# k's first tile among the products of the first stage, and the first modulation's sums shared out anew

## The chip, the cores and the metric

The kernel runs on one core of one Trainium2 chip. The metric is the time of one execution in microseconds on the device (us): the median of the timed runs. A core has TensorE (matmuls, below PE; its weight loads PEld), VectorE (DVE), ScalarE (ACT), GpSimd (POOL) and SyncE (SP, which here only issues transfers from memory). Each engine works through its own list in order and waits where something it needs is not there. Matmuls add up in PSUM, which has 8 banks; everything else lies in SBUF.

## The reference

One decoder block on x of 512 tokens by 1024 features, all in float32: a modulation vector from c, an RMS norm with scale and shift, nine projections of it, retention over q, k, v with rotary phases, a short gated convolution of b, c and u, a gated merge, and an FFN. What bears on this change:

```python
mod = silu(c) @ ada_w + ada_b                       # 6 x 1024: shift, scale, gate (mixer), the same (FFN)
h = rmsnorm(x, norm_mix_g) * (1 + sc_m) + sh_m      # 512 x 1024
q, k, v, g_ret, b_cv, c_cv, u_cv, g_a, g_b = split(h @ w_in, 9)
q, k = rope(q), rope(k)                             # cos and sin of positions * inv_freq
u = c_cv * u_cv                                     # then three taps, times b_cv
```

## The kernel before

*Products in three parts.* Every matrix product is made of reduced-precision parts: a float32 tensor is split into a high part (`_h`, a cast on ScalarE) and a low part (`_l`, a subtraction, mostly on VectorE), and three products are added, low by high, high by low, and high by high. For the normed input these are `Hh` and `Hl`, for weights `w_.._h` and `w_.._l`.

*The first stage* (lines 330 to 512) runs while the weights of the modulation still arrive. x comes in four tiles, is squared and scaled, and is turned by TensorE (`tx`) into `xT`, features on partitions: eight slices of 128 features. A slice can be modulated only when the sums of `ada_w` over c for its features are there. So the features go in pairs of slices j = 0, 2, 4, 6. `ada_load("m", j)` brings the shift and scale columns of the pair as 8 transfers of 256 KB, and `w_load(j)` the pair's rows of w_in for the first two column tiles of c, u and b.

*The modulation of a pair.* Its 8 raw rows are weighted with silu(c). `ada_sum` and `some_sums` do it on VectorE, one instruction for a row of 512 values (`acc_m`); four small matmuls with ones then add over the partitions (`mod_m<-ones,acc_m`). For pair 0, `mod_first` lets TensorE take rows 0, 1, 2, 3 and 7 directly from the raw weights, and VectorE sums rows 4 to 6. `mod_cols` makes shift `s_m` and scale `a_m` from the result; `h_hi` applies them on ScalarE, twice, once rounded into `Hh` and once in full; `h_lo` makes `Hl` on VectorE.

*The products of slice k* (`products(k)`) are 18 matmuls: six groups (two tiles each of c, u and b), each with three parts. All six groups stay in PSUM from slice 0 to slice 7: four banks called `acc`, two called `pv`; two more, `aux`, hold the modulation sums. `busy(n)` are matmuls whose result nobody reads.

*What sets the order.* In this stage the order is written out by hand: with `strict`, each engine's instruction is issued behind the one before it in the program. In the loop over j, 8 products of slice j-1 come ahead of pair j's sums and 10 behind them.

*Behind the stage* a scheduler orders each engine's list. v of the first head pair is projected (`value_proj`), then k (`proj`, two tiles of 24 matmuls), q and the gate. VectorE meanwhile computes the rotary phases (`rotary`, tiles `fr`, `fy`, `ft`); ScalarE makes their sines and cosines (`ropeC`, `ropeS`) behind a table load; `rope` applies them to k and q; then come the scores (`st`) of retention, which need the split k and q. For the second head pair the low part of v's weights is made by GpSimd. Raw weights lie in three buffers (`raw`), split ones in four each (`hi`, `lo`), and projections in the four `acc` banks, each in rotation.

Of the kernel before, what the change touches and what calls it, by code (L numbers as in the profile page):

```python
# [70 lines left out]
def block_kernel(ctx, tc, x, c, positions, ada_w, ada_b, norm_mix_g, w_in, conv_w, ret_w_out,  # L71
# [143 lines left out]
    def mod_cols(f, j, n, pt):  # L215

        r1 = R_ADA + ADA["sh_" + f] // P + j
        g0 = (R_GM if f == "m" else R_GF) + j
        for k in range(j, j + n):
            i = k - j  # L220
            vec.scalar_tensor_tensor(mod["a_" + f][:, k:k + 1], pt[:, n + i:n + i + 1],
                                     vecs[0][:, g0 + i:g0 + i + 1], mod["b_" + f][:, k:k + 1],
                                     ALU.mult, ALU.add)
            if k == j:
                vec.tensor_tensor(mod["s_" + f][:, j:j + n], pt[:, 0:n], vecs[0][:, r1:r1 + n],
                                  ALU.add)
# [8 lines left out]
    def mod_vecs(f, j, a=None):  # L235

        pt = aux(f"mod_{f}{j}")
        a = ada_sum(ada_raw.pop((f, j)), 4 * P, f"{f}{j}") if a is None else a
# [3 lines left out]
        mod_cols(f, j, 2, pt)  # L242


    def half_ss(part, s, h, name):
# [62 lines left out]
    def x_load():  # L308
        for t in range(NT):
            xt = wp.tile([P, 2, S], F32, tag="hi", name=f"x_{t}")  # L310
            xs[t] = [xt[:, h] for h in range(2)] + [xt.rearrange("p h n -> p (h n)")]
            load_raw.last = sync.dma_start(xs[t][2], x[0, t * P:(t + 1) * P, :])

    def w_load(k):
        for n in "cub":
            w_raw[n, k] = scr(f"w_{n}0_{k}", F32, [P, 2, 2 * P])
            load_raw.last = sync.dma_start(
                w_raw[n, k], wi[k * P:(k + 2) * P, COL[n]:COL[n] + 2 * P].rearrange(
                    "(k p) n -> p k n", p=P))

    pe.strict = pool.strict = act.strict = vec.strict = sync.strict = True
# [33 lines left out]
    mod01 = []  # L355

    def mod_first(k, tiles=(0, 1)):

        for j in tiles:
            for i in range(2):  # L360
                c0 = 2 * i * P + j * P
                mm(mod01[j][:, i:i + 1], lhsT=ada_raw["m", 0][k][:, c0:c0 + P], rhs=cs[:, k:k + 1],
                   start=k == 0 and i == 0, stop=False)

    def mod_sums(a, j):
        for i in range(2):
            c0 = 2 * i * P + j * P
            mm(mod01[j][:, i:i + 1], lhsT=a[:, c0:c0 + P], rhs=ones32[:, 0:1],
               start=False, stop=i == 1)
# [14 lines left out]
    transpose(tr[:, 0:P], rows, ident)  # L384
    x_squares(3)
    rows_by_feature(tr)
    mod01 += [aux(f"mod_m{j}") for j in range(2)]
    mod_first(0)
    x_scaled(2)
    busy(1)  # L390
    x_by_feature(1, 0, act.copy)
    x_by_feature(1, 1, vec.tensor_copy)
    mod_first(1)
    busy(1)
    mod_first(2)
# [12 lines left out]

    grp = [(n, i) for n in "cub" for i in range(2)]
    gps = {}  # L410
    for i, g in enumerate(grp):
        gps[g] = acc(f"p_{g[0]}0{g[1]}") if i < 4 else pv(f"p_{g[0]}0{g[1]}")
    wt, raws = {}, {}
    hist = []
    hlast = []

    def w_hi(n, k):
        raws[n, k] = w_raw.pop((n, k))
        wt[n, k] = [slot(f"w_{n}0_{k}_{z}", F32R, [P, 2, 2 * P]) for z in "hl"]
# [54 lines left out]
    busy(2)
    mod_first(7, (1,))
    mod_sums(a, 1)
    mod_cols("m", 1, 1, mod01[1])
    w_lo("u", 0)
# [154 lines left out]
    def proj(src, col, Ah, Al, name, eng=None):  # L633
        raw = load_raw(src, 0, KT, col, 2 * P, "w_" + name)
        for i in range(2):
            wh, wl = split(raw[:, :, i * P:(i + 1) * P], [P, KT, P], f"w_{name}{i}", eng)
            yield i, fm_gemm(acc(f"p_{name}{i}"), wh, wl, Ah, Al)
            tick()

    def gate_proj(p):  # L640
        for i in range(2):
            gate_split(p, i)
            wh, wl = gate_w.pop((p, i))
            yield i, fm_gemm(acc(f"p_g{p}{i}"), wh, wl, Hh, Hl)
            tick()
# [65 lines left out]
    for p in range(H // 2):  # L711
        kk, qq, vv, gg = {}, {}, {}, {}
        for i, pt in value_proj(p, pool if p == 1 else None):
            value(pt, f"v{p}{i}", vv, i)
        if p == 0:
            rope_tables()
        for i, pt in proj(wi, COL["k"] + 2 * p * P, Hh, Hl, f"k{p}"):
            kk[i] = rope(pt, f"k{p}{i}")
        for i, pt in proj(wi, COL["q"] + 2 * p * P, Hh, Hl, f"q{p}"):
            qq[i] = rope(pt, f"q{p}{i}")  # L720
        retention(p, kk, qq, vv, gg)
        for i, pt in gate_proj(p):
            gg[i] = slot(f"g{p}{i}")
            act.activation(gg[i], pt, AF.Silu)
# [296 lines left out]
```

## Time and profile before

| | us |
|---|---|
| median of 3 runs | 973.99 (972.45 to 975.49) |
| the profiled execution | 971.54 |
| its span, first to last instruction | 969.7 |
| TensorE busy in the span | 954.5 (98%) |
| VectorE busy | 558.7 (58%) |
| ScalarE busy | 340.0 (35%) |
| GpSimd busy | 15.2 (2%) |
| TensorE's mean granted clock | 0.995 of full speed |

Busy shares are averages over the whole span. Matmuls are pipelined, so the time of one as shown (0.39 us) is longer than the distance between the starts of two. The stage that the change touches is the first 62 us.

### The profile page before, as it was taken

What the parts mean: (1) busy time and instruction counts of PE and PEld (TensorE: products, weight loads), DVE (VectorE), ACT (ScalarE), POOL (GpSimd) and SP (SyncE); (2) the same over time, 40 slices, a digit from 0 to 9 for tenths busy, and PEclk for the clock granted to TensorE, in tenths of its full rate; (3) what the DMA queues carried; (4) which work ended last, traced back from release to release, by engine and by line L of the source; (5) the groups of instructions that cost most, each with busy time, mean ns of one, the idle gap of its engine ahead of it and who ended that gap; (6) DMA issues with size and microseconds to landing.
All of it is one profiled execution on the core that took longest, in us unless ns stands there. A gap on an engine that the chain in (4) does not pass through costs nothing.

```text
span 969.7 us, 11383 instructions
## 1 busy us (share of the span) xinstructions
PE 954.5 (98%) x4651; PEld 807.2 (83%) x4651; DVE 558.7 (58%) x836; ACT 340.0 (35%) x502; POOL 15.2 (2%) x22
## 2 busy tenths in 40 slices
PE   8899999999999999999999998999999999999997
PEld 8788989888888888888888887988888888888886
DVE  4888875959775755554574458356533433333354
ACT  7434434444543423222233336422322122222223
POOL 2001000000000000000000002000000000000000
PEclk9999999999999999999999999999999999999999
DMA  9953332141322146764553541235423222331302
GB/s 310 312 167 109 98 98 98 55 142 41 102 87 87 59 129 192 218 184 153 174 174 115 188 131 55 95 115 166 157 90 128 87 87 88 118 121 66 109 1 87
DMA packets 107956, 120.98 MB, mean 125 GB/s; under 512 B 3636, under 2 KB 95840, under 8 KB 107904
## 3 DMA queue, kind: packets, MB, share of 16 engines
q1 hardware_dynamic: 107680, 120.08, 39.3%
q8 instruction: 36, 0.59, 0.3%
q0 software_dynamic: 224, 0.18, 0.1%
q14 instruction: 16, 0.13, 0.0%
HBM read 118.15 MB, written 2.10 MB: 124 GB/s over the span
## 4 chain that ended last, share of the span: by engine, by line
PE 95%; DVE 2%; ACT 1%; DMA 1%; issue 1%; SPq 0%; ACTq 0%; DVEq 0%
PE p_fu L64 12%; PE p_fg L64 12%; PE dn L64 12%; PE p_v L64 5%; PE p_ga L64 5%; PE p_k L64 5%; PE p_q L64 5%; PE p_g L64 5%; PE p_gb L64 5%; PE p_yb L64 4%; PE p_ya L64 4%; PE mix L64 4%; PE p_u L64 3%; PE p_b L64 3%; PE p_c L64 3%; PE y L64 2%
## 5 line engine op out<-in xcount | busy, mean ns | idle before, releaser
L64 PE MATMUL p_fu<-Gl,w_fu_h 128*128 128x512 f32 (+1 forms) x192 | 71.4, 372 | 0.0
L64 PE MATMUL p_fu<-Gh,w_fu_l 128*128 128x512 f32 (+1 forms) x192 | 71.3, 371 | 0.0
L64 PE MATMUL p_fu<-Gh,w_fu_h 128*128 128x512 f32 (+1 forms) x192 | 71.3, 371 | 0.0
L64 PE MATMUL dn<-w_dn_h,fa_l 128*128 128x512 f32 (+1 forms) x176 | 67.5, 384 | 0.0
L64 PE MATMUL dn<-w_dn_l,fa_h 128*128 128x512 f32 (+1 forms) x176 | 67.4, 383 | 0.0
L64 PE MATMUL dn<-w_dn_h,fa_h 128*128 128x512 f32 (+1 forms) x176 | 67.4, 383 | 0.0
L64 PE MATMUL p_fg<-Gh,w_fg_l 128*128 128x512 f32 x160 | 62.3, 389 | 0.0
L64 PE MATMUL p_fg<-Gl,w_fg_h 128*128 128x512 f32 x160 | 62.3, 389 | 0.0
L64 PE MATMUL p_fg<-Gh,w_fg_h 128*128 128x512 f32 x160 | 62.3, 389 | 0.0
L64 DVE TENSOR_TENSOR w_dn_l<-w_dn,w_dn_h 128x1024 fp32r<-128x1024 f32 x22 | 26.9, 1224 | 57.5 <-ACT w_dn_h L64 57.5
L64 DVE TENSOR_TENSOR w_fg_l<-w_fg,w_fg_h 128x1024 fp32r<-128x1024 f32 x20 | 24.5, 1224 | 56.5 <-ACT w_fg_h L64 56.5
L64 ACT CAST w_fu_h<-w_fu 128x1024 fp32r<-128x1024 f32 x22 | 23.2, 1053 | 73.0 <-PE p_fu L64 40.1
L64 ACT CAST w_dn_h<-w_dn 128x1024 fp32r<-128x1024 f32 x22 | 23.1, 1050 | 65.6 <-PE dn L64 39.4
L64 DVE TENSOR_TENSOR fg<-p_fu,fg 128x512 f32<-128x512 f32 x22 | 15.2, 691 | 49.8 <-PE p_fu L64 49.8
L64 PEld LDWEIGHTS p_fu<-Gh,w_fu_h 128*128 128x128 f32 x192 | 36.2, 188 | 6.3
L64 PEld LDWEIGHTS p_fu<-Gl,w_fu_h 128*128 128x128 f32 x192 | 36.2, 188 | 6.2
L64 PEld LDWEIGHTS p_fu<-Gh,w_fu_l 128*128 128x128 f32 x192 | 36.2, 188 | 6.1
L64 ACT ACTIVATE fg<-p_fg 128x512 f32<-128x512 f32 x22 | 13.2, 598 | 80.0 <-PE p_fg L64 80.0
L64 PEld LDWEIGHTS dn<-w_dn_h,fa_l 128*128 128x128 f32 x176 | 33.1, 188 | 6.5
L64 PEld LDWEIGHTS dn<-w_dn_h,fa_h 128*128 128x128 f32 x176 | 33.1, 188 | 6.5
L64 PEld LDWEIGHTS dn<-w_dn_l,fa_h 128*128 128x128 f32 x176 | 33.1, 188 | 6.5
L64 PE MATMUL p_v<-w_v_h,Hh 128*128 128x256 f32 x128 | 36.2, 283 | 0.0
(329 smaller groups left out, 2523.7 us busy)
## 6 DMA issues: line engine op xcount, KB each, us to landing
w_fg<-in_ffn_w_gate_dram SPq DMA_DIRECT2D x11, 1024.0 KB, 5.4
w_fu<-in_ffn_w_up_dram SPq DMA_DIRECT2D x11, 1024.0 KB, 5.6
w_dn<-in_ffn_w_down_dram SPq DMA_DIRECT2D x10, 1024.0 KB, 5.0
ada_m<-in_ada_w_dram SPq DMA_DIRECT2D x32, 256.0 KB, 6.0
ada_f<-in_ada_w_dram SPq DMA_DIRECT2D x32, 256.0 KB, 4.5
w_v<-in_w_in_dram SPq DMA_DIRECT2D x4, 1024.0 KB, 6.0
w_k<-in_w_in_dram SPq DMA_DIRECT2D x4, 1024.0 KB, 5.1
w_q<-in_w_in_dram SPq DMA_DIRECT2D x4, 1024.0 KB, 5.1
```

The costliest lines, as they stand in the source:

```text
L64: self.last = op(*args, **kw)
```

## The change

*k in the first stage.* `w_load` also brings the pair's rows of w_in for k's first tile (128 columns, 128 KB). Its high and low parts are made like the others', and `products(k)` has 21 matmuls instead of 18. The seventh group's bank `kp` (tile `p_k00`) is one of the two `aux` banks; the other one, `mods`, serves the modulation sums of all pairs. While pair 0's sums are made, `kp` lends two columns to them. Behind the stage, `first_k` hands over `kp` as k's first tile and loads and multiplies only the second one (`w_k01`, 512 KB, 24 matmuls).

*The sums.* For pair 0 TensorE takes rows 0, 1 and 7, and VectorE sums rows 2 to 6, row 6 in two halves. For pair 2 TensorE also takes row 7, and VectorE rows 0 to 6. For pairs 4 and 6 VectorE still sums all eight.

*The order.* 14 products of slice j-1 come ahead of pair j's sums, and 7 behind. The low parts of u, b and k of a pair come behind the second slice's modulation in the program. The numbers of `busy` matmuls around pair 0 change.

```diff
     def w_load(k):
-        for n in "cub":
-            w_raw[n, k] = scr(f"w_{n}0_{k}", F32, [P, 2, 2 * P])
+        for n in "cubk":
+            cols = P if n == "k" else 2 * P
+            w_raw[n, k] = scr(f"w_{n}0_{k}", F32, [P, 2, cols])
...
+    kp, mods = aux("p_k00"), aux("mods")
+
+    def mod_row(j, k, banks, first, cols=range(4)):
+
+        for i in cols:
+            mm(banks[i % 2][:, i:i + 1], lhsT=ada_raw["m", j][k][:, i * P:(i + 1) * P],
+               rhs=cs[:, k:k + 1], start=first and (i == 0 or i == 1 and banks is apart), stop=False)
...
+    apart, both = (mods, kp), (mods, mods)
...
-    mod_first(3)
-    a = ada_sum(ada_raw["m", 0][4:7], 4 * P, "m0", None, 4)
+    mod_row(0, 1, apart, False)
+    a = ada_sum(ada_raw["m", 0][2:6], 4 * P, "m0", None, 2)
     x_by_feature(3, 0, act.copy)
     x_by_feature(3, 1, act.copy)
-    busy(2)
-    mod_first(7, (0,))
-    mod_sums(a, 0)
+    for i in range(2):
+        c0 = slice(2 * i * P, 2 * (i + 1) * P)
+        ada_sum([ada_raw["m", 0][6][:, c0]], 2 * P, "", a[:, c0], 6)
+    busy(5)
+    mod_row(0, 7, apart, False, (0, 1, 2))
+    mod_sums(a, apart, False, (0, 2))
+    mod_row(0, 7, apart, False, (3,))
+    mod_sums(a, apart, False, (1, 3))
+    busy(4)
...
-    some_sums(2, 2, 4)
+    some_sums(2, 2, 7)

     for j in range(2, KT, 2):
...
         steps = products(j - 1)
-        run(steps, 8)
-        some_sums(j, 4, KT)
-        for n in "cub":
+        run(steps, 14)
+        if j == 2:
+            mod_row(j, 7, both, True)
+        else:
+            some_sums(j, 4, KT)
+        for n in "cubk":
             w_hi(n, j)
+        mod_sums(sums[j], both, j > 2)
         w_lo("c", j)
-        mod_vecs("m", j, sums[j])
-        w_lo("u", j)
-        w_lo("b", j)
-        h_hi(j)
-        h_hi(j + 1)
-        run(steps, 10)
+        mod_cols("m", j, mods)
+        for k in (j, j + 1):
+            h_hi(k)
+            h_full(k)
+        for n in "ubk":
+            w_lo(n, j)
+        run(steps)
...
+    def first_k():
+
+        yield 0, kp
+        wh, wl = split(load_raw(wi, 0, KT, COL["k"] + P, P, "w_k01"), [P, KT, P], "w_k01")
+        yield 1, fm_gemm(acc("p_k01"), wh, wl, Hh, Hl)
+        tick()
...
-        for i, pt in proj(wi, COL["k"] + 2 * p * P, Hh, Hl, f"k{p}"):
+        for i, pt in proj(wi, COL["k"] + 2 * p * P, Hh, Hl, f"k{p}") if p else first_k():
```

TensorE's list around the sums of the second modulation, before; `acc_m_354` is VectorE's sum over pair 2's rows, `mod_m_398` its bank:

```order
L62 MATMUL p_b_287<-Hh,w_b_0_l 128x512
L62 MATMUL p_b_288<-Hh,w_b_0_l 128x512
L62 MATMUL p_c_283<-Hh,w_c_0_h 128x512
L62 MATMUL p_c_284<-Hh,w_c_0_h 128x512
L62 MATMUL mod_m_398<-ones_84,acc_m_354 128x1 x4
L62 MATMUL p_u_285<-Hh,w_u_0_h 128x512
```

And now; `p_k_126` is `kp`, `ada_m_4_324` holds pair 2's raw rows 4 to 7:

```order
L62 MATMUL p_u_293<-Hh,w_u_0_h 128x512
L62 MATMUL p_b_294<-Hh,w_b_0_h 128x512
L62 MATMUL p_b_295<-Hh,w_b_0_h 128x512
L62 MATMUL p_k_126<-Hh,w_k_0_h 128x512
L62 MATMUL mods<-cs,ada_m_4_324 128x1 x4
L62 MATMUL mods<-ones_84,acc_m_362 128x1 x4
L62 MATMUL p_c_290<-Hl,w_c_0_h 128x512
```

The sums stood behind the first two of slice 1's high products and now stand behind all of its products with `Hh`, and row 7's four matmuls stand ahead of them.

ScalarE's list from the weights of v to the first sine, before; `w_v`, `w_k`, `w_q` and `w_g` are the first head pair's weights:

```order
L64 CAST w_v_h<-w_v_618 128x1024
L64 CAST w_k_h<-w_k_805 128x1024 x2
L64 COPY c_663<-p_c_283 128x512
L64 COPY c_664<-p_c_284 128x512
L64 CAST w_q_h<-w_q_885 128x1024 x2
L64 CAST w_g_h<-w_g_967 128x1024
L64 CAST v_h<-v_c 128x512 x2
L64 CAST w_g_h<-w_g_967 128x1024
L64 ACT_TABLE_LOAD
L64 ACTIVATE ropeC<-fr 64x256
```

And now; `w_v_1059` is the second head pair's:

```order
L64 CAST w_v_h<-w_v_663 128x1024
L64 CAST w_k_h<-w_k_860 128x1024
L64 CAST w_q_h<-w_q_901 128x1024
L64 COPY c_708<-p_c_290 128x512
L64 COPY c_709<-p_c_291 128x512
L64 CAST w_q_h<-w_q_901 128x1024
L64 CAST w_g_h<-w_g_983 128x1024
L64 CAST v_h<-v_c 128x512
L64 CAST w_g_h<-w_g_983 128x1024
L64 CAST v_h<-v_c 128x512
L64 CAST w_v_h<-w_v_1059 128x1024
L64 ACT_TABLE_LOAD
```

One cast of k's weights is gone, q's and the gate's stand further ahead, and the second head pair's first cast of `w_v`, which stood behind the sines, now stands ahead of the table load.

## Rows read from the trace of the kernel before

**Rows 1.** Stretches: us; busy PE, PEld, DVE, ACT, POOL; clock, DMA share, GB/s

```profile
25.00:30.00 5.00, 2.25 (x11) 1.55 (x9) 4.82 (x8) 1.85 (x3) 0.00 (x0) 1.00 1.09 348
30.00:35.00 5.00, 5.00 (x21) 4.15 (x22) 4.42 (x10) 3.53 (x5) 0.00 (x0) 0.73 1.09 348
```

**Rows 2.** Timeline of TensorE, first stage: start, length, instruction, idle before and releaser

```profile
18.34 0.58 PE L62 MATMUL mod_m<-ones,acc_m 128*128 128x1 f32 x4
...
20.58 0.70 PE L62 MATMUL p_c<-Hh,w_c_h 128*128 128x512 f32 x2
...
29.90 1.05 PE L62 MATMUL mod_m<-ones,acc_m 128*128 128x1 f32 x8 [2.75 <-DVE acc_m L62]
...
33.99 1.05 PE L62 MATMUL p_c<-Hh,w_c_l 128*128 128x512 f32 x2
...
50.31 1.02 PE L62 MATMUL mod_m<-ones,acc_m 128*128 128x1 f32 x8 [0.38 <-DVE acc_m L62]
...
61.73 0.28 PE L64 MATMUL p_v<-w_v_h,Hl 128*128 128x256 f32 x1
```

**Rows 3.** Timeline of VectorE in the same stage

```profile
14.79 0.49 DVE L62 TENSOR_SCALAR acc_m<-ada_m,cs 128x512 f32<-128x512 f32 x1 [2.05 <-DMA ada_m<-in_ada_w_dram]
...
16.32 0.75 DVE L62 SCALAR_TENSOR_TENSOR acc_m<-ada_m,cs,acc_m 128x512 f32<-128x512 f32 x1 [0.26 <-DMA ada_m<-in_ada_w_dram]
...
25.16 4.68 DVE L62 SCALAR_TENSOR_TENSOR acc_m<-ada_m,cs,acc_m 128x512 f32<-128x512 f32 x6
...
36.36 3.11 DVE L62 SCALAR_TENSOR_TENSOR acc_m<-ada_m,cs,acc_m 128x512 f32<-128x512 f32 x4
...
47.05 3.10 DVE L62 SCALAR_TENSOR_TENSOR acc_m<-ada_m,cs,acc_m 128x512 f32<-128x512 f32 x4
...
55.74 0.69 DVE L62 TENSOR_TENSOR Hl<-xT,Hh 128x512 fp32r<-128x512 f32 x1 [1.67 <-ACT xT L62]
56.35 2.35 DVE L64 TENSOR_TENSOR w_v_l<-w_v,w_v_h 128x1024 fp32r<-128x1024 f32 x2
```

**Rows 4.** Chain of waits, 60 to 140 us: start, length, what

```profile
61.89 11.51 PE p_v L64 x96
73.40 10.91 PE p_k L64 x48
84.31 10.88 PE p_q L64 x48
```

**Rows 5.** Who waited for whom, 60 to 120 us: total, times, longest

```profile
PEld st L64 <- DVE q_l L64: 0.2, 1, 0.2
```

**Rows 6.** Timeline of VectorE, 61 to 106 us

```profile
61.82 1.22 DVE L64 TENSOR_TENSOR w_k_l<-w_k,w_k_h 128x1024 fp32r<-128x1024 f32 x1
...
87.33 0.43 DVE L62 TENSOR_SCALAR fr<-fr 128x512 f32<-128x512 f32 x1
90.44 0.69 DVE L64 TENSOR_TENSOR k_a<-p_k,ropeC 128x512 f32<-128x512 f32 x1 [2.69 <-ACT ropeC L64]
...
93.17 1.71 DVE L64 TENSOR_TENSOR k_a<-k_a,k_b 128x512 f32<-128x512 f32 x1
...
96.94 2.89 DVE L64 TENSOR_TENSOR k_a<-k_a,k_b 128x512 f32<-128x512 f32 x1
...
105.31 0.69 DVE L64 TENSOR_TENSOR q_l<-q_a,q_h 128x512 fp32r<-128x512 f32 x1
```

**Rows 7.** Timeline of ScalarE, 84 to 88 us

```profile
84.40 1.05 ACT L64 CAST w_g_h<-w_g 128x1024 fp32r<-128x1024 f32 x1 [1.74 <-PE p_k L64]
85.47 1.28 ACT L64 ACT_TABLE_LOAD   x1
87.79 0.42 ACT L64 ACTIVATE ropeC<-fr 64x256 f32<-64x256 f32 x1 [1.03 <-DVE fr L62]
```

**Rows 8.** Timeline of GpSimd, 60 to 330 us

```profile
91.93 2.40 POOL L64 TENSOR_TENSOR w_v_l<-w_v,w_v_h 128x1024 fp32r<-128x1024 f32 x1 [85.98 <-ACT w_v_h L64]
96.57 2.71 POOL L64 TENSOR_TENSOR w_v_l<-w_v,w_v_h 128x1024 fp32r<-128x1024 f32 x1 [2.24 <-ACT w_v_h L64]
```

More of the change, by code (lines that the diff above doesn't have):

```diff
@@ L213, in ada_load, with mod_scale, mod_shift, mod_cols @@
             pieces += [raw[:, q].rearrange("p s n -> p (s n)") for q in range(4)]
[L215 to L226, printed above, removed]
+    def mod_scale(f, k, col):
+        g = (R_GM if f == "m" else R_GF) + k
+        vec.scalar_tensor_tensor(mod["a_" + f][:, k:k + 1], col, vecs[0][:, g:g + 1],
+                                 mod["b_" + f][:, k:k + 1], ALU.mult, ALU.add)
+    def mod_shift(f, k, cols, n):
+        r = R_ADA + ADA["sh_" + f] // P + k
+        vec.tensor_tensor(mod["s_" + f][:, k:k + n], cols, vecs[0][:, r:r + n], ALU.add)
+    def mod_cols(f, j, pt):
+        mod_scale(f, j, pt[:, 2:3])
+        mod_shift(f, j, pt[:, 0:2], 2)
+        mod_scale(f, j + 1, pt[:, 3:4])
     def mod_gains(f):
@@ L233, in mod_gains, with mod_vecs @@
                                  ALU.add, ALU.mult)
-    def mod_vecs(f, j, a=None):
+    def mod_vecs(f, j):
         pt = aux(f"mod_{f}{j}")
-        a = ada_sum(ada_raw.pop((f, j)), 4 * P, f"{f}{j}") if a is None else a
+        a = ada_sum(ada_raw.pop((f, j)), 4 * P, f"{f}{j}")
         for i in range(4):
@@ L241, in mod_vecs @@
                start=True, stop=True)
-        mod_cols(f, j, 2, pt)
+        mod_cols(f, j, pt)
     def half_ss(part, s, h, name):
@@ L353, in x_by_feature, with mod_sums @@
             copy(xT[2 * h + q][:, :, t * P:(t + 1) * P], txs[t, h][:, 2 * q:2 * q + 2])
[L355 to L369, printed above, removed]
+    kp, mods = aux("p_k00"), aux("mods")
[3 more added lines that the diff above has]
+               rhs=cs[:, k:k + 1], start=first and (i == 0 or i == 1 and banks is apart), stop=False)
+    def mod_sums(a, banks, first, cols=range(4)):
+        for i in cols:
+            mm(banks[i % 2][:, i:i + 1], lhsT=a[:, i * P:(i + 1) * P], rhs=ones32[:, 0:1],
+               start=first and i == 0, stop=i == 3 or i == 2 and banks is apart)
+    apart, both = (mods, kp), (mods, mods)
     x_load()
@@ L386, in block_kernel @@
     rows_by_feature(tr)
-    mod01 += [aux(f"mod_m{j}") for j in range(2)]
-    mod_first(0)
     x_scaled(2)
@@ L392, in block_kernel @@
     x_by_feature(1, 1, vec.tensor_copy)
-    mod_first(1)
-    busy(1)
-    mod_first(2)
+    mod_row(0, 0, apart, True)
     x_scaled(3)
@@ L400, in block_kernel @@
     mod_gains("m")
-    mod_first(3)
-    a = ada_sum(ada_raw["m", 0][4:7], 4 * P, "m0", None, 4)
+    mod_row(0, 1, apart, False)
+    a = ada_sum(ada_raw["m", 0][2:6], 4 * P, "m0", None, 2)
     x_by_feature(3, 0, act.copy)
     x_by_feature(3, 1, act.copy)
-    busy(2)
-    mod_first(7, (0,))
-    mod_sums(a, 0)
+    for i in range(2):
[7 more added lines that the diff above has]
+    busy(4)
     grp = [(n, i) for n in "cub" for i in range(2)]
-    gps = {}
-    for i, g in enumerate(grp):
-        gps[g] = acc(f"p_{g[0]}0{g[1]}") if i < 4 else pv(f"p_{g[0]}0{g[1]}")
+    gps = {g: (pv if g[0] == "b" else acc)(f"p_{g[0]}0{g[1]}") for g in grp}
+    grp.append(("k", 0))
+    gps["k", 0] = kp
     wt, raws = {}, {}
@@ L418, in w_hi @@
         raws[n, k] = w_raw.pop((n, k))
-        wt[n, k] = [slot(f"w_{n}0_{k}_{z}", F32R, [P, 2, 2 * P]) for z in "hl"]
+        wt[n, k] = [slot(f"w_{n}0_{k}_{z}", F32R, raws[n, k].shape) for z in "hl"]
         act.copy(wt[n, k][0], raws[n, k])
@@ L430, in h_hi, with h_full @@
         h32[k] = xT[k // 2][:, k % 2]
-        av, sv = mod["a_m"][:, k:k + 1], mod["s_m"][:, k:k + 1]
-        hist.append(act.activation(Hh[:, k, :], h32[k], AF.Identity, scale=av, bias=sv))
-        act.activation(h32[k], h32[k], AF.Identity, scale=av, bias=sv)
+        hist.append(act.activation(Hh[:, k, :], h32[k], AF.Identity,
+                                   scale=mod["a_m"][:, k:k + 1], bias=mod["s_m"][:, k:k + 1]))
+    def h_full(k):
+        act.activation(h32[k], h32[k], AF.Identity, scale=mod["a_m"][:, k:k + 1],
+                       bias=mod["s_m"][:, k:k + 1])
     def h_lo(k):
@@ L447, in products @@
         ops = []
-        parts = (1, 0, 2) if k == 0 else (0, 1, 2)
+        parts = (0, 1, 2) if k % 2 else (1, 0, 2)
         for part in parts:
@@ L457, in products, with run @@
         if k == 0:
-            order = {"c": 0, "u": 1, "b": 2}
-            ops = sorted(ops[:12], key=lambda o: order[o[4][0]]) + ops[12:]
+            order = {"c": 0, "u": 1, "b": 2, "k": 3}
+            ops = sorted(ops[:14], key=lambda o: order[o[4][0]]) + ops[14:]
         for o, w, x, (first, last), _ in ops:
             yield mm(o, lhsT=w, rhs=x, start=first, stop=last)
-    def run(steps, n):
+    def run(steps, n=21):
         for _, _ in zip(range(n), steps):
             pass
+    for k in range(2):
+        mod_scale("m", k, apart[k][:, 2 + k:3 + k])
+        mod_shift("m", k, apart[k][:, k:k + 1], 1)
     w_hi("c", 0)
-    mod_cols("m", 0, 1, mod01[0])
     h_hi(0)
@@ L472, in block_kernel @@
     w_hi("u", 0)
+    w_lo("u", 0)
     w_hi("b", 0)
[L474 to L478, printed above, removed]
+    w_lo("b", 0)
+    h_full(0)
+    w_hi("k", 0)
+    w_lo("k", 0)
     h_hi(1)
@@ L481, in block_kernel @@
     w_load(2)
-    w_lo("b", 0)
     h_lo(0)
-    busy(2)
-    run(products(0), 18)
+    h_full(1)
+    run(products(0))
     act.copy(blkr, blk)
@@ L496, in block_kernel @@
         steps = products(j - 1)
-        run(steps, 8)
-        some_sums(j, 4, KT)
-        for n in "cub":
+        run(steps, 14)
[4 more added lines that the diff above has]
+        for n in "cubk":
             w_hi(n, j)
+        mod_sums(sums[j], both, j > 2)
         w_lo("c", j)
-        mod_vecs("m", j, sums[j])
-        w_lo("u", j)
-        w_lo("b", j)
-        h_hi(j)
-        h_hi(j + 1)
-        run(steps, 10)
+        mod_cols("m", j, mods)
[5 more added lines that the diff above has]
+        run(steps)
         some_sums(j + 2, 0, 2)
         h_lo(j)
-        run(products(j), 18)
+        run(products(j))
         some_sums(j + 2, 2, 4)
         h_lo(j + 1)
-    run(products(KT - 1), 18)
+    run(products(KT - 1))
     pe.strict = pool.strict = act.strict = vec.strict = sync.strict = False
```

2 lines of the change are left out of this document (1 added, 1 removed).

## The prediction

> **What bounds the kernel now.** I read the busy table by stretches first, to see where TensorE is not full; then the timelines of TensorE and VectorE in those stretches; then the chain of waits, to see what the time after them hangs on.
>
> The chain is TensorE nearly everywhere, so time can only come from holes in it. In [rows 1] the stretch from 25 to 30 us has 2.25 us of matmul in 5 us, and the next one a granted clock of 0.73. [Rows 2] show why: the sums of the second modulation, at 29.90, stood 2.75 us until VectorE had finished the vector they read (six rows from 25.16, 4.68 us, end 29.84, [rows 3]). Shortly after, two products take 0.85 us start to start (33.14, 33.99, 34.84; the row at 33.99 is one) instead of 0.45: TensorE was granted the lower of its two levels, 1.2 GHz. Four such pairs cost about 1.6 us. The first product starts at 20.58, the first one of v at 61.73. The 144 products of the stage, at 0.2273 (10.91 us for 48 products of k, [rows 4]), are 32.7 of these 41.15 us.
>
> From 61.9 on TensorE has no hole for 48 us [rows 4]. But one row says how little is behind that: the first scores' weights waited 0.2 us for q_l of VectorE [rows 5], written from 105.31 to 106.00 [rows 6]. At that place VectorE is exactly as late as TensorE. Whatever moves TensorE forward before it is kept only as far as VectorE's chain (rotary fr, ScalarE's sines, rope of k and q) moves too. That is the second thing to work out.
>
> **The first stage.** All times are on the trace's clock.
>
> *Start.* Rows 2 and 3 of the first modulation leave TensorE (16 matmul instructions) and go to VectorE, which waited there 2.05 us for row 4 [rows 3]: 0.49 + 0.76 us, done before row 4 lands. Row 6 is bound by its transfer (start 16.32, [rows 3]); in two halves it ends near 17.1. TensorE took the sums only at 18.34 [rows 2], since its queue was that long; now it has them at 17.1. The first shift and scale come 1.2 us earlier, and the first product, behind four dummies, at about 19.15 instead of 20.58: 1.4 us. Cover: if row 6 lands late, this goes.
>
> *Second modulation.* In front of its sums stand 35 products instead of 26: 19.15 + 35 x 0.2273 = 27.1, less than 0.1 us of waits for k's low part included. Then row 7 on TensorE, some 0.9 us, 28.0. VectorE starts its six rows earlier by the 1.4 us and does five (one row, 0.78 us, less), against 0.4 us for k's low part (half of 0.69, with its fixed part): 29.84 - 1.4 - 0.8 + 0.4 = 28.0. The hole closes, and with it I take the low clock away. The sums end at 28.9 instead of 30.95.
>
> *Each further pair.* VectorE took 9.6 and 10.7 us from sum to sum (ends 29.84, 39.47, 50.15 in [rows 3]); with k's part 10.0, the 10.7 having held a wait for TensorE. TensorE needs 42 x 0.2273 + 0.85 = 10.4 and now sets the pace. A pair's transfers are 2.88 MB, with k's 0.13 MB 3.01; at 348 GB/s [rows 1] 8.7 us, so they stay hidden; if a packet of half the length took as long as a whole one, 9.0. Two pairs: the last sums end at 28.9 + 20.8 = 49.75, against 51.33 [rows 2].
>
> *End.* Behind them stand 49 products, 11.1 us: v starts at 60.9 instead of 61.73, though 24 products of k are now done. The last Hl followed the end of the sums by 4.4 us and v's first low part that by 0.6 (55.74 and 56.35 in [rows 3]) in an order that has not changed, so VectorE reaches v's low parts at 54.8: 1.57 us earlier.
>
> TensorE is thus ahead by 0.85 + 24 x 0.2273 = 6.3 us when it reaches q. From the start of v it took 44.2 us to the scores (v 11.51, k 10.91, then q with 10.88 and the gate alike, [rows 4]); it would reach them at 60.9 + 44.2 - 5.45 = 99.65.
>
> **The chain to the scores.** VectorE's work from v's low parts to the last fr row ran 56.35 to 87.76 [rows 3, 6] with 0.2 us of waiting. One of the two splits of w_k (1.14 us start to start, the row at 61.82) falls away: the last fr ends at 54.8 + 30.1 = 84.9. ScalarE now casts w_v of the second head pair ahead of its table load: it waits there for TensorE's first q tile (60.9 + 22.67 = 83.57, as the cast of w_g waited at 84.40, [rows 7]), then 1.05 cast and 1.28 table: sines from 85.95 instead of 87.79, 1.84 us earlier.
>
> That cast also starts GpSimd's subtraction earlier. In [rows 8] it runs 2.40 us from 91.93 and 2.71 from 96.57, and in [rows 6] the sums k_a, with both operands in SBUF, take 1.71 and 2.89 us where 0.69 is usual: both end 0.55 us behind GpSimd. Those two holds cost 3.3 us of the chain. Now the first subtraction runs from 84.76 to 87.2, beside the sines, when VectorE has just finished fr and is idle. The second follows the cast behind the sines, 90.2 to 92.7, and holds the first sum, ready at 91.3, for 1.4 us.
>
> Rope then: first product with the table at 85.95 + 2.65 = 88.6, first k's three rows and the second's first 2.7 us, hold and sum to 93.25, then 2.65 us for the second k (94.9 to 96.94 and one sum of 0.6), and 5.6 us (before 6.2, one row of q's rope now standing behind) to the end of q_l: 101.5 against 106.0. Gain 4.5 us. TensorE, 6.3 us ahead, waits some 0.4 us for the second gate's bank and 1.2 us at the scores; the remaining gain stays, as the rows behind move with both engines.
>
> **Sum.** The profiled execution took 971.54 us, span 969.7 and 1.84 around it; 971.54 - 4.5 = 967.0. It lies 2.45 us under the median of the three timed runs, 973.99; on that scale the forecast is 973.99 - 4.5 = 969.5.
>
> **A rule against it.** The margin in which fr's last row gets ahead of GpSimd is small: it starts near 84.5, GpSimd near 84.76. [Rows 6, 8] show holds only for rows with two SBUF operands; the last fr row has one. The Trainium skill (GPSIMD Engine Reference, Key points) says that the interface is shared also with VectorE instructions in a two-port mode. No row here shows that. What it would make of the time is the first rival, and the trace so far neither supports nor excludes it.
>
> **Rivals.**
> *1. GpSimd goes first and holds the end of fr.* Two or three tenths are enough, and several terms above are known no better. Then fr ends at 87.6, the sines start at 87.65, rope at 90.3; the second subtraction, 91.8 to 94.3, holds the sum ready at 93.0; q_l ends at 103.1: gain 2.9 us, 971.1. For it: the small margin. Against: v's start and VectorE's end hang on the same sums, so their distance (6.1 us) moves little. If the split of w_g is held as well (VectorE 0.7 us later), another 1.6 us go: gain 1.3, 972.7.
>
> *2. VectorE's chain is no bound*, because fewer holds remain than I count. Then TensorE keeps its 6.3 us: 967.7. Against: the 0.2 us of [rows 5], and that VectorE waited only 0.2 us in the 31.4 before the sines.
>
> *3. Nothing.* k's products lengthen the stage instead of filling its holes, since waits for transfers take the place of that for VectorE: the rows of the modulations come at the pace of [rows 1], and VectorE would want those of the second 1.9 us earlier. With 1.1 us lost at each of the four sums everything behind moves by 4.5: v from 65.4, q_l to 106.0, and the time is 974.0. Against: VectorE read six rows without a wait at 25.16.
>
> *4. Slower: the low clock lasts.* Place: the first stage. TensorE has new short waits at 16 to 17 us, and from 28 on a small one before each of the three sums. At the lower level a product costs 0.2 us more [rows 2]. As TensorE now stands ahead of VectorE's next work (the sums are behind 14 products instead of 8), each loss there moves VectorE too. Against a gain of 4.5 us it decides from 23 products on; 38 (some 16 us at the lower level) make the kernel 3 us slower, 977. For it: the clock did fall in this stage. Against: it fell behind a gap of 2.75 us and not behind the short one ahead of 50.31.
>
> **How the numbers follow.** The main sum has 0.5, rival 1 0.23 (0.06 of it with the deeper hold), rival 2 0.07, rival 3 0.11, rival 4 0.09. A difference under 0.3% (2.9 us) can't be told from none here. Faster: nearly all of the main sum (0.46), half of rival 1's 2.9 (0.09), rival 2 (0.07), together 0.62. Slower by more than that: most of rival 4, 0.08. The rest, 0.30, is no difference. Range: rival 2 with the runs' scatter of 1.2 us down, 966.5; up past both forms of rival 1 to 973.4. The main sum's own range is 968 to 971.
>
> **What would show it.** Right: the first product near 19.2; no wait over 0.5 us ahead of the second modulation's sums, clock 1.00 throughout; v from 60.9; sines from 86; a wait of about 1 us at the scores that names q_l or q_h. Rival 1: an fr row of over 2 us beside GpSimd, sines past 87.5. Wrong altogether: a first product not before 20.3, a clock under 0.9 in any stretch of the stage, or rows of the second modulation waiting for transfers.

## The result and the profile after

The changed kernel takes 967.46 us (median of four runs, 966.55 to 968.20), against 974.74 for the four runs of the kernel before that stand beside it: ratio 0.9941, interval 0.9916 to 0.9966. The forecast was 969.5. The profiled execution took 968.18 us, span 966.4, against 971.54 and 969.7: 3.3 us less, where 4.5 were forecast.

Each run lists its span and its mean granted clock, and the two must be read together, since both kernels scatter by their clock. At .995, the clock of both profiled executions, before has spans of 967.8 to 970.4 (17 of the 47 runs of it that stand beside the experiments, median 969.5), the changed kernel 966.0 to 967.4 (seven of its 16, experiments included, median 966.4). That is 3.1 us at equal clock. In both profiled executions the clock was low at two places, before at 32 to 36 us and 598 to 603, the changed kernel at 18 to 22 us and 595 to 599, so hardly anything of the 3.1 us is clock. The medians differ by more because before falls lower: 18 of those 47 runs have a clock of .990 or less, none of the 16 of the changed kernel.

First the stretches of the changed kernel (us; busy PE, PEld, DVE, ACT, POOL; clock, DMA share, GB/s). They answer to [rows 1].

```profile
16.00:17.00 1.00, 0.82 (x8) 0.70 (x6) 0.96 (x3) 0.00 (x0) 0.00 (x0) 1.00 1.16 364
17.00:18.00 1.00, 0.86 (x7) 0.78 (x7) 0.52 (x3) 0.62 (x1) 0.00 (x0) 1.00 1.04 321
18.00:19.00 1.00, 1.00 (x7) 1.00 (x7) 0.35 (x3) 0.67 (x1) 0.00 (x0) 0.57 1.12 335
19.00:20.00 1.00, 1.00 (x6) 1.00 (x6) 1.00 (x4) 1.00 (x3) 0.00 (x0) 0.50 1.10 350
...
21.00:22.00 1.00, 1.00 (x5) 0.82 (x4) 0.79 (x2) 0.97 (x3) 0.00 (x0) 0.72 1.09 347
...
25.00:30.00 5.00, 5.00 (x29) 4.30 (x27) 3.34 (x5) 2.17 (x4) 0.00 (x0) 1.00 1.10 343
30.00:35.00 5.00, 5.00 (x27) 4.24 (x27) 4.07 (x10) 3.15 (x4) 0.00 (x0) 1.00 1.09 347
```

The hole at 25 to 30 us is closed (5.00 us of matmul, before 2.25) and the low clock behind it is gone (1.00, before 0.73). But TensorE has a new low stretch, from 18 to 22 us, at 0.50, which is 1.2 GHz.

The timeline of TensorE shows what it hit; it answers to [rows 2].

```profile
17.12 0.78 PE L62 MATMUL mods<-ones,acc_m 128*128 128x1 f32 x4 [0.30 <-DVE acc_m L62]
...
18.70 2.06 PE L62 MATMUL idle<-ident 128*128 128x128 f32 x8
20.41 1.20 PE L62 MATMUL p_c<-Hh,w_c_h 128*128 128x512 f32 x2
...
29.82 1.03 PE L62 MATMUL mods<-ones,acc_m 128*128 128x1 f32 x8
```

The first sums start at 17.12 as forecast. Then the low clock doubles the dummies ahead of the first product (2.06 us for these eight instructions), so that this starts at 20.41, where 19.15 was forecast. The sums of the second modulation, at 29.82, wait for nothing.

VectorE in the same stage, beside [rows 3]:

```profile
15.01 2.45 DVE L62 SCALAR_TENSOR_TENSOR acc_m<-ada_m,cs,acc_m 128x512 f32<-128x512 f32 x4 [0.33 <-DMA ada_m<-in_ada_w_dram]
...
23.94 3.90 DVE L62 SCALAR_TENSOR_TENSOR acc_m<-ada_m,cs,acc_m 128x512 f32<-128x512 f32 x5
27.76 0.69 DVE L62 TENSOR_TENSOR w_c_l<-w_c,w_c_h 128x512 fp32r<-128x512 f32 x1
30.89 0.22 DVE L62 SCALAR_TENSOR_TENSOR a_m<-mods,vecs,b_m 128x1 f32<-128x1 f32 x1 [2.45 <-PE mods L62]
```

Its five rows end at 27.84 (forecast 28.0), and now it is VectorE that waits for TensorE, 2.45 us. The sides have changed.

The chain of waits after that (start, length, what), which answers to [rows 4]:

```profile
62.97 11.51 PE p_v L64 x96
74.48 5.47 PE p_k L64 x24
79.95 5.45 PE p_q L64 x24
...
85.47 1.05 ACT w_v_h L64
86.54 1.28 ACT L64
87.84 0.42 ACT ropeC L64
...
103.17 0.74 PE st L64 x2
```

TensorE has only one tile of k left to do and reaches the end of q's first tile at 85.40. There the chain leaves it: ScalarE's cast of w_v for the second head pair waits for that tile, behind the cast stands the table load, behind that the sines, then VectorE's rotary rows. VectorE and GpSimd in that stretch, beside [rows 6] and [rows 8]:

```profile
86.34 0.43 DVE L62 TENSOR_SCALAR fr<-fr 128x512 f32<-128x512 f32 x1
90.49 0.69 DVE L64 TENSOR_TENSOR k_a<-p_k,ropeC 128x512 f32<-128x512 f32 x1 [3.72 <-ACT ropeC L64]
...
93.23 1.77 DVE L64 TENSOR_TENSOR k_a<-k_a,k_b 128x512 f32<-128x512 f32 x1
...
97.07 0.68 DVE L64 TENSOR_TENSOR k_a<-k_a,k_b 128x512 f32<-128x512 f32 x1
...
102.42 0.69 DVE L64 TENSOR_TENSOR q_l<-q_a,q_h 128x512 fp32r<-128x512 f32 x1
```

```profile
86.66 2.40 POOL L64 TENSOR_TENSOR w_v_l<-w_v,w_v_h 128x1024 fp32r<-128x1024 f32 x1 [80.71 <-ACT w_v_h L64]
92.06 2.40 POOL L64 TENSOR_TENSOR w_v_l<-w_v,w_v_h 128x1024 fp32r<-128x1024 f32 x1 [3.00 <-ACT w_v_h L64]
```

The first k_a sum stands beside GpSimd's second subtraction and takes 1.77 us; the second, beside nothing, 0.68 (before 1.71 and 2.89). q_l ends at 103.11, before 106.00. And the waits of TensorE's weights from 60 to 120 us (total, times, longest), where [rows 5] had 0.2:

```profile
PEld st L64 <- DVE q_l L64: 1.1, 1, 1.1
PEld p_g L64 <- DVE k_b L64: 0.6, 1, 0.6
```

TensorE's weights wait 1.7 us in all, 1.1 of them at the scores and 0.6 ahead of a gate tile. From 85.40 TensorE has 16.3 us of products to the scores and would be there at 101.7; its product with q_l starts at 103.17. Two questions are left: what the three parts of the change (earlier sums, k's tile, the clock) are worth each, and what the wait at the scores costs.

### The profile page after: what moved, and what is told of

Same layout as the page of the kernel before. It is cut to its first block, busy times and chain, and to the rows that moved or that the text cites. A ratio compares the mean times of both kernels' runs of the same rounds, so it can differ in the third digit from the quotient of the medians.

```text
span 966.4 us, 11389 instructions
## 1 busy us (share of the span) xinstructions
PE 953.5 (99%) x4647; PEld 807.1 (84%) x4647; DVE 556.9 (58%) x841; ACT 340.9 (35%) x505; POOL 14.9 (2%) x22
## 4 chain that ended last, share of the span: by engine, by line
PE 94%; DVE 2%; DMA 1%; ACT 1%; issue 0%; SPq 0%; ACTq 0%; DVEq 0%
PE p_fu L64 12%; PE p_fg L64 12%; PE dn L64 12%; PE p_v L64 5%; PE p_ga L64 5%; PE p_gb L64 5%; PE p_yb L64 5%; PE p_ya L64 5%; PE mix L64 4%; PE p_q L64 4%; PE p_k L64 4%; PE p_g L64 3%; PE p_u L64 3%; PE p_b L64 3%; PE p_c L64 3%; PE y L64 2%
```

## The experiments

Ten kernels, in three groups that ran together. The table has the median, the ratio to before with its interval, and the spans by mean clock.

| kernel | us | ratio | .998, .999 | .996, .997 | .992 to .995 |
|---|---|---|---|---|---|
| e1_after | 967.98 | 0.9951 [0.9935, 0.9967] | | 964.6 to 965.0 (4) | 966.0 to 968.0 (8) |
| e2_fill | 966.47 | 0.9935 [0.9912, 0.9958] | 963.1 to 964.3 (3) | 965.1 to 966.2 (3) | |
| e3_nok | 967.06 | 0.9943 [0.9920, 0.9965] | | 964.6 to 965.3 (4) | 966.1, 966.2 |
| e4_old_sums | 968.96 | 0.9967 [0.9945, 0.9989] | | 966.6 to 968.0 (6) | 966.3 to 967.8 (4) |
| f5_warm_sine | 967.52 | 0.9932 [0.9917, 0.9947] | | 965.5 to 965.8 (5) | 967.0 |
| g_one | 965.65 | 0.9912 [0.9895, 0.9929] | 962.4, 962.4 | 963.6, 964.1 | 965.5, 965.6 |
| g_warm_one | 964.77 | 0.9904 [0.9887, 0.9920] | 962.2 to 963.0 (3) | 963.7, 964.4 | |
| g_nok_one | 967.75 | 0.9931 [0.9914, 0.9947] | | 964.8 to 965.8 (3) | 966.2 to 966.6 (3) |
| h_nok_fill | 967.20 | 0.9948 [0.9929, 0.9967] | 963.5 to 963.7 (3) | 965.4 to 966.3 (5) | |
| h_fu_vec | 961.91 | 0.9900 [0.9875, 0.9925] | 959.7 to 961.0 (6) | | |

e4_old_sums had two more runs, at .987 and .988 (973.2 and 973.5). The medians of before were 972.33 (e1 to e4), 974.36 (f5 to g_nok_one) and 971.66 (the last two), so between groups the spans at equal clock are compared. Even these are not the same: before has, at .995, medians of 969.7, 970.0 and 968.6 in the three groups, so that some 1 us between kernels of two groups is not shown by spans alone.

**e1_after: the changed kernel again.**

> The changed kernel unaltered, to see how its time varies. My theory: the first stage gains some 5 us of TensorE time, of which about 3 us reach the scores, because the second stage's chain (ScalarE's cast and table load, the sines, VectorE's rotary rows, q_l) moves less than TensorE; and a stretch of low TensorE clock at 18 to 21 us, after short waits at 16 to 17 us, costs some 1.5 us in about half of the runs. Expected: spans of either about 964.9 (clock .997) or about 966.4 (clock .995), gain 3.3 to 4.9 us over before. Rival 1 (all of the gain is k's 24 products in the holes) and rival 2 (all of it is the low clock at 32 to 36 us of before that is gone) expect the same time here.

Both kinds of run came, four at .997 (964.6 to 965.0) and eight at .992 to .995. The profiled one fell to 1.2 GHz at two places, 18 to 22 us and between 593 and 600 us. A run with none of the two would be near .999, with one near .997.

**e2_fill: the wait at 17 us filled.**

```
     mod_row(0, 7, apart, False, (0, 1, 2))
+    busy(2)
```

> After, with two more dummy pieces on TensorE between its last row of the first modulation and the first sums, so that the wait at 16.7 to 17.1 us is filled. My theory: the granted clock stays at 1.00 from 15 to 25 us, the first product starts at about 19.3 instead of 20.4, and every run is of the quicker kind: span about 964.9 at .997, some 1.5 us less than after's profiled run. Rival (the low stretch at 18 to 21 comes by chance and not from the gaps): both kinds of run remain, with a span of 966.4 in some; and if the dummies themselves come late the first product moves 0.3 to 0.5 us later.

The stretches of e2_fill, first the stage, then the other place:

```profile
15.00:20.00 5.00, 5.00 (x44) 4.95 (x44) 3.65 (x10) 2.05 (x5) 0.00 (x0) 1.00 1.10 343
20.00:25.00 5.00, 5.00 (x22) 3.78 (x22) 4.29 (x8) 3.87 (x8) 0.00 (x0) 1.00 1.09 348
590.00:600.00 10.00, 7.55 (x61) 7.01 (x60) 9.61 (x15) 6.23 (x12) 2.50 (x2) 1.00 0.32 106
```

and of e1_after:

```profile
15.00:20.00 5.00, 4.76 (x34) 4.44 (x33) 3.88 (x11) 2.82 (x5) 0.00 (x0) 0.85 1.10 344
20.00:25.00 5.00, 5.00 (x19) 4.02 (x18) 4.61 (x8) 2.66 (x6) 0.00 (x0) 0.80 1.09 348
590.00:600.00 10.00, 7.56 (x46) 6.96 (x45) 9.60 (x15) 6.25 (x13) 2.92 (x2) 0.83 0.33 106
```

The clock stayed at 1.00 in the first stage, and no run was below .996; the median is 1.5 us lower, as expected. The first product starts at 19.74, not 19.3, as the first sums come later, at 17.69. This is not the dummies' doing: TensorE had waited 0.50 us at 13.4 us, ahead of them, and had everything behind that later. At the other place TensorE is as idle in both (7.55 and 7.56), and fell in one of the two: there chance decides, as far as these runs show. In the first stage it isn't settled either. Of the changed kernel, with k's tile, new sums and no fill, 10 of 16 runs are at .995 or less; of the five kernels that have the fill besides, 3 of 29 (3 of 23 without h_fu_vec, which has no wait at 593 us). But g_nok_one, below, has the same dummies and fell, and the wait of 0.50 us at 13.4 us was followed by no low clock.

**e3_nok: the sums without k's tile.**

```
-        for n in "cubk":
-            cols = P if n == "k" else 2 * P
+        for n in "cub":
+            cols = 2 * P
...
-        run(steps, 14)
+        run(steps, 12)
...
-        for i, pt in proj(wi, COL["k"] + 2 * p * P, Hh, Hl, f"k{p}") if p else first_k():
+        for i, pt in proj(wi, COL["k"] + 2 * p * P, Hh, Hl, f"k{p}"):
```

> After without k's first tile in the first stage: three pieces (c, u, b) and so six banks, 18 products a slice, and k projected whole after v as before; the new sharing of the sums between TensorE and VectorE stays. My theory: the earlier sums alone give 2 to 2.5 us over before (the hole at the second modulation's sums shrinks but VectorE's rows then leave TensorE short of products), and k's tile the other 1 to 2.5 us. Rival 1 (all of the gain is k): no gain over before. Rival 2 (all of it is the low clock that is gone): the same time as after.

The expectation fell: without k's tile the kernel is as fast as with it, in the median and at equal clock. The reason stands in the end of e3_nok's chain:

```profile
91.60 10.88 PE p_g L64 x48
102.48 0.68 PE st L64 x3
```

and in that of e1_after:

```profile
79.41 5.45 PE p_q L64 x24
...
102.63 0.73 PE st L64 x2
```

In e3_nok TensorE reaches the scores at 102.48 and waits for nothing. In e1_after q's first tile ends at 84.9; with 16.3 us of products behind it TensorE is there at 101.2, 1.3 us earlier, and waits for q_l until 102.63. So the new sums alone close the hole, and what k's tile gives beyond that is spent in the wait at the scores. ScalarE's order differs too. Without k's tile the sines stand ahead of the second head pair's cast of w_v, as before the change, and start 2.4 us earlier than in e1_after (87.29):

```profile
84.87 0.42 ACT L64 ACTIVATE ropeC<-fr 64x256 f32<-64x256 f32 x1 [1.70 <-DVE fr L62]
```

What this order costs by itself no run shows; f5_warm_sine, below, brings the sines forward again and gains nothing. Rival 1 (no gain without k's tile) is out. Rival 2 (only the clock) expects this time too, and the next kernel has to decide on it.

**e4_old_sums: k's tile with the sums shared as before.**

```
...
-    mod_row(0, 1, apart, False)
-    a = ada_sum(ada_raw["m", 0][2:6], 4 * P, "m0", None, 2)
+    mod_row(0, 3, apart, False)
+    a = ada_sum(ada_raw["m", 0][4:7], 4 * P, "m0", None, 4)
...
-        if j == 2:
-            mod_row(j, 7, both, True)
-        else:
-            some_sums(j, 4, KT)
+        some_sums(j, 4, KT)
...
```

> After with k's first tile kept, but with the sums shared as before: TensorE sums rows 0 to 3 and 7 of the first modulation and none of the second pair's rows, VectorE rows 4 to 6 and all eight. My theory: the first product at about 20.5, TensorE waits some 1.4 us for the second modulation's sums, v starts at about 63.5, and the gain over before is about 2.5 us. Rival 1 (all of the gain is k): the same time as after, within 0.5 us. Rival 2 (only the clock): as before if the low clock at 32 to 36 us comes back, as after if not.

The hole is there, 1.14 us, and so is the low clock behind it (0.73 from 30 to 35 us). The sums of the second modulation on TensorE:

```profile
30.07 1.05 PE L62 MATMUL mods<-ones,acc_m 128*128 128x1 f32 x8 [1.14 <-DVE acc_m L62]
```

v starts at 64.84 (63.5 expected), and the median is 3.4 us under before (2.5 expected). In the medians k's tile alone gives 3.4 us, the sums alone (e3_nok) 5.3, both together 4.4: the two are no sum, they fill the same hole. At .997, where before has only two runs (967.9 and 968.4), the three gains are some 1.2, 3 and 3.3 us; there the sums alone give nearly the whole. As this kernel is some 1.2 us under before at that clock, with a low clock behind the hole in both, the gain is not only the clock (rival 2); and it is 2 us above e1_after, so not only k's tile (rival 1). Equal mean clock is no perfect measure, though: the four runs of this kernel at .994 and .995 are no longer than its six at .996 and .997, and can't be told from e1_after's. This kernel and before, the two with the hole, are also the only ones with runs at .990 or less: 2 of 12 and 18 of 47, against none of 65 of all the others.

The next kernels ask what the wait at the scores costs. In the four kernels with k's tile and unchanged second part (the changed one, e1, e2, e4) the time from the start of ScalarE's cast of w_v to the scores' product with q_l is 17.70, 17.70, 17.69 and 17.69 us. It moves as a whole with the end of q's first tile. The kernels from here on have e2_fill's dummies too.

**f5_warm_sine: the table loaded ahead of that cast.**

```
     def rope_tables():
+        with tc.issue_after(act.last.ins):
+            sin_warm.append(act.activation(ropeC[:, 0:1], eps_t, AF.Sin))
...
+            with tc.issue_after(sin_warm[0].ins):
```

> After with the two dummies that fill TensorE's wait at 17 us (as in e2_fill), and the Sin table loaded early: one dummy sine behind v's second cast, ahead of the cast of the second head pair's w_v, which waits for q's first tile. My theory now: in every kernel with k's tile in the first stage the scores start 17.70 us after TensorE ends q's first tile (that cast, table load, sines, rotary rows, q_l), so TensorE's own lead of 1.3 us from k's tile is lost in a wait there. Here the sines start when fr is ready, about 85.8 (86.85 in e2_fill), but VectorE's first k_a sum is still held until GpSimd's second subtraction ends, at about 93.5 instead of 94.0: scores at most 0.5 us earlier, span 963.5 to 964.0 in runs of clock .999. Rival (the table load alone is the bound): 1.0 us less, 963.0.

No gain is there at equal clock (965.5 to 965.8 in four runs at .997, against 965.1 in two of e2_fill, of another group), where 0 to 0.5 us less were expected. VectorE in e2_fill:

```profile
91.64 0.69 DVE L64 TENSOR_TENSOR k_a<-p_k,ropeC 128x512 f32<-128x512 f32 x1
92.24 1.78 DVE L64 TENSOR_TENSOR k_a<-k_a,k_b 128x512 f32<-128x512 f32 x1
```

and here, with GpSimd beside it:

```profile
90.13 0.69 DVE L64 TENSOR_TENSOR k_a<-p_k,ropeC 128x512 f32<-128x512 f32 x1
90.74 2.69 DVE L64 TENSOR_TENSOR k_a<-k_a,k_b 128x512 f32<-128x512 f32 x1
```

```profile
90.48 2.38 POOL L64 TENSOR_TENSOR w_v_l<-w_v,w_v_h 128x1024 fp32r<-128x1024 f32 x1 [2.94 <-ACT w_v_h L64]
```

The sum is ready 1.5 us earlier than in e2_fill (0.5 us of it because TensorE was earlier in this execution) and held 0.9 us longer (2.69 for 1.78). The rest went into the order, since a row of q's rotary work (0.7 us) now stands ahead of q_l: the scores' wait is 1.3 us. The price of a changed order was the term that the expectation lacked.

**g_one: the second low part of w_v on VectorE.**

```
-            ws = [split(raw[:, 4 * s:4 * s + 4, :], [P, 4, 2 * P], f"w_v{p}{s}", eng)
+            ws = [split(raw[:, 4 * s:4 * s + 4, :], [P, 4, 2 * P], f"w_v{p}{s}", None if s else eng)
```

> As e2_fill, but the second of the two w_v low parts of the second head pair is subtracted by VectorE and no longer by GpSimd; the table load stays where it is. My theory: VectorE's first k_a sum takes 0.7 instead of 1.8 us, q_l and the scores come 1.1 us earlier (101.1 instead of 102.18), span 962.9 at clock .999. Rival (a subtraction of 1.2 us more on VectorE costs what the hold did): no change, 964.0.

The sum on VectorE, then two rows of the chain:

```profile
91.88 0.68 DVE L64 TENSOR_TENSOR k_a<-k_a,k_b 128x512 f32<-128x512 f32 x1
```

```profile
84.12 1.06 ACT w_v_h L64
...
100.72 0.74 PE st L64 x2
```

The hold is gone, and 17.7 us have become 16.6 (84.12 to 100.72). Spans at .999 are 962.4 (two runs) against 963.1 to 964.3 of e2_fill, in another group: 0.7 to 1.9 us less, 1.1 expected. So the hold was on the path; the 1.1 us rest on the trace more than on the spans.

**g_warm_one: both.** f5_warm_sine's and g_one's edits together.

> Both edits together (early Sin table, second low part on VectorE) on top of e2_fill. My theory: VectorE's chain is then 2.1 us shorter, so TensorE sets the pace alone and starts the scores at about 100.6; gain over e2_fill 1.5 us, span 962.5 at clock .999, and no wait of TensorE for q_l or k_b is left. Rival (TensorE's wait at the scores is not what lies on the path): span as e2_fill, 964.0.

Now the chain is TensorE without a break from v to the scores, and TensorE waits nowhere on the way; only its weights wait 0.4 us for q_l, beside a product. Spans at .999 are 962.2 to 963.0 (962.5 expected). With the hold gone the early table brings little more, 964.77 against 965.65 in the median, nothing at equal clock.

**g_nok_one and h_nok_fill: what k's tile is worth when the chain is short.** g_one without k's tile, then with four dummies in place of two.

> As g_one, but without k's tile in the first stage (as in e3_nok). e3_nok's TensorE never waited at the scores, so shortening VectorE's chain gives nothing there. My theory: only the low clock at 18 to 21 us goes, spans of about 963.7 at .999 and 965.0 at .997, that is 0.5 to 1.3 us above g_warm_one: what k's tile is worth shows only when the chain behind it is short. Rival (k's tile is worth nothing on TensorE either): the same time as g_warm_one.

g_nok_one fell to the low clock at 18 to 22 us in its profile and in three of six runs, so it can't be compared in the median:

```profile
16.00:17.00 1.00, 0.95 (x10) 0.86 (x9) 0.96 (x3) 0.00 (x0) 0.00 (x0) 1.00 1.12 352
17.00:18.00 1.00, 0.98 (x11) 0.90 (x9) 0.52 (x3) 0.62 (x1) 0.00 (x0) 1.00 1.06 340
...
20.00:21.00 1.00, 1.00 (x4) 0.81 (x4) 1.00 (x3) 1.00 (x3) 0.00 (x0) 0.50 1.10 349
```

> As g_nok_one, but with four dummies more than after, not two, ahead of the first sums, since TensorE there still fell to the low clock at 19 to 22 us. What it is for: k's worth at an equal clock. My theory: the clock stays at 1.00 from 15 to 25 us, the first sums move 0.3 us later, spans of about 963.8 at .999 and 965.0 at .997, which is some 1.2 us above g_warm_one (962.2 to 963.0 at .999) and equal to e2_fill. Rival 1 (k's tile is worth nothing on TensorE, and g_nok_one was slower by its clock alone): 962.5 at .999. Rival 2 (the dummies have no part in the clock): spans of 966.1 to 966.6 at .995 in half of the runs.

Three runs at .999 have spans of 963.5 to 963.7 (963.8 expected), by the medians 1.4 us above those of g_warm_one (1.2 expected) and level with e2_fill. This compares two groups. Within one group, at .996 and .997, g_nok_one (964.8 to 965.8) stands against g_one and g_warm_one (963.6 to 964.4), 1.6 us by the medians, and the traces of e3_nok and e1_after gave 1.3. So k's tile is worth some 1.4 us on TensorE; in the kernel as changed the chain to the scores eats all of it. None of the eight runs is at .995 or less, against three of six with two dummies, which speaks against rival 2, though on another chip.

**h_fu_vec: the same hold elsewhere.** g_warm_one with the two low parts of w_fu on VectorE.

```
-            ws.append(split(raw[:, :, i * P:(i + 1) * P], [P, KT, P], f"w_fu0{i}", pool))
+            ws.append(split(raw[:, :, i * P:(i + 1) * P], [P, KT, P], f"w_fu0{i}"))
```

> As g_warm_one, with the two low parts of w_fu also subtracted by VectorE, so that GpSimd does nothing beside VectorE after 88 us. In all kernels a 128x1 sum of VectorE (n_r, 2.32 us from 590.0 in g_warm_one) stands beside GpSimd's second w_fu subtraction, and TensorE waits 2.4 us for xn behind it; in some of the runs the clock falls after that wait. My theory: n_r's sum takes 0.16 us, and Gl's two rows 1.29 in place of 2.39, but two subtractions of 1.14 us and one of w_fg stand ahead of xn now: TensorE waits about 1.5 us, span 0.5 to 1.0 us less than g_warm_one, 961.5 at .999. Rival (the subtractions cost what the hold did): no change, 962.3 at .999.

VectorE, GpSimd and TensorE in g_warm_one, then VectorE and TensorE in h_fu_vec:

```profile
590.02 2.32 DVE L64 TENSOR_TENSOR n_r<-n2s 128x1 f32<-128x1 f32 x1
589.83 2.49 POOL L64 TENSOR_TENSOR w_fu_l<-w_fu,w_fu_h 128x1024 fp32r<-128x1024 f32 x1 [0.89 <-ACT w_fu_h L64]
593.43 1.09 PE L900 MATMUL tx<-ident,xn 128*128 128x128 f32 x8 [2.43 <-DVE xn L64]
```

```profile
588.22 0.15 DVE L64 TENSOR_TENSOR n_r<-n2s 128x1 f32<-128x1 f32 x1
591.98 1.09 PE L900 MATMUL tx<-ident,xn 128*128 128x128 f32 x8
```

A sum of 128x1 had taken 2.32 us beside GpSimd, and TensorE had waited 2.43 us for what follows it. In h_fu_vec no product of TensorE waits there any more (1.5 us were expected), the clock is 1.00 from 590 to 600 us, and all six runs lie at .998 or .999, with spans of 959.7 to 961.0 (961.5 expected). With 961.91 us this is the fastest kernel of the study.

The hold is only a part of that. From the end of the products `mix` to the transposes `tx` of xn it is 4.15 us in g_warm_one (589.28 to 593.43) and 3.38 in h_fu_vec (588.60 to 591.98): VectorE's side became 0.8 us shorter, as the expectation had it. The rest of the wait went because TensorE's own list came out in another order: 27 products of the FFN's gate (`p_fg`, 0.12 us each) stand ahead of `tx`, where g_warm_one, as before the change, has 11. The expectation did not have this, and no run separates the two.

## Why the prediction was right, and where it was off

**The main sum held in its mechanism; that its number is near is partly luck.** These steps are in the trace: the hole and the clock at 30 us, a TensorE that sets the pace of the pairs (10.56 and 10.42 us from sum to sum, forecast 10.4), one GpSimd hold instead of two, and a lead that ends in waits ahead of the scores (1.7 us, forecast 1.6). But two of the three signs that the prediction set for being wrong altogether came too: a first product not before 20.3, and a clock under 0.9 in the stage. The time measured, 967.46, lies under the 968 to 971 of the main sum. Two errors work against each other in it: between the profiled executions the gain was 1.2 us smaller than forecast, between the medians 2.8 us larger.

**The step that failed is the first product at 19.15.** It came at 20.41. VectorE's part and the start of the sums were in time; the four dummies and the first products ran at 1.2 GHz. What comes after is late by 1.6 to 1.9 us: the second modulation's sums at 29.82 (28.0), v at 62.81 (60.9), the sines at 87.84 (85.95), the end of q_l at 103.11 (101.5). In e2_fill, at clock 1.00, q_l ends at 102.13; its first sums had come 0.6 us later than forecast, behind another wait, and without that q_l would be at the forecast's 101.5. So the low clock accounts for the lateness, as far as two executions show. The main sum had taken the low clock away with the hole and had put the short waits at 16 to 17 us at nothing. Rival 4 had named these waits; what it got wrong is that the low clock lasts: after 22 us it is 1.00 for the rest of the stage.

**The bound of the second part was right in size, and said too narrowly.** The prediction said that the gain is kept only as far as VectorE's chain moves. But fr was ready 1.1 us before the table was loaded, and the chain hangs on ScalarE's cast behind q's first tile, on TensorE. It moves with TensorE, with a fixed length to the end of q_l: from 83.57 to 101.5 in the forecast's numbers, 17.9 us, and 17.6 in the trace.

**The rivals.** 1 (GpSimd goes first) didn't occur: the last fr row started at 86.34 and took 0.43 us, GpSimd started at 86.66, a margin of 0.3 us, as worked out. That the sines came past 87.5, one of its signs, has the other reason given above. 2 (VectorE's chain is no bound) has the time nearest to the one measured, 967.7, and the wrong reason: TensorE does wait, and g_one and g_warm_one get back what it loses. 3 (transfers) is out: ahead of the second sums VectorE's wait is for TensorE.

**What the forecast lacked** is that many runs of before have a lower clock than the profiled one. The counts above (.990 or less only in the two kernels with the hole) point to the hole at 27 to 30 us as the cause; no run at such a clock was profiled, so this is not shown. On the medians of the first four runs each the gain was 7.3 us, in e1_after's group 4.4; at equal clock 3.1.

On the hold, the Trainium skill (SBUF — State Buffer, section "SBUF: two separate sides") says that VectorE and GpSimd have a pair of ports that one of them gets for a whole instruction, that a VectorE operation with two SBUF inputs takes it against a GpSimd operation that reads SBUF, and that the other blocks. The trace agrees: the sum of 128x1 took 2.32 us beside a subtraction of 2.49, and k_a from PSUM, at 91.64 in e2_fill, the usual 0.69, though GpSimd was subtracting from 91.07 to 93.47.

## What to carry to other kernels

When a hole is filled in an early stage, follow the lead that it gives to the next place where the engine meets another one's chain, and work out how long that chain is from the point where it leaves the engine: here it was fixed at 17.7 us, and k's tile, on top of the new sums, was worth nothing until the chain was made shorter. Look in such a chain for short VectorE rows that take as long as a GpSimd instruction beside them; moving one of 1.2 us to VectorE shortened VectorE's own chain by 1.1 us. After such an edit compare the lists of the other engines too: in h_fu_vec a part of the gain came from TensorE's order.

## What the runs showed of the hardware

TensorE's clock fell to 1.2 GHz after waits of a few tenths of a us (busy 0.82 and 0.86 in two stretches of 1 us), in g_nok_one after 0.95 and 0.98; in g_one the same two stretches were 0.90 and 0.99 busy, and the clock stayed at 1.00. After the same wait of 2.4 us at 593 us it fell in some executions and not in others. The spans at .997 are 1.0 to 1.8 us longer than those at .999 (medians in five kernels, before among them, some of one run). Which gap brings the fall about is left open. In h_fu_vec's profile TensorE has no wait from 20 us to 960, and none of its six runs is under .998.
